# A fifth buffer for the high and the low halves of weights, paid for with two of the 36 large tiles

## The chip, the cores and the metric

One NeuronCore of one Trainium2 chip runs the whole layer in one launch. The metric is device time in microseconds (us) of that core. The kernel before takes 1455.81 us, the median of 3 runs (1452.03 to 1458.66). Engines are named as the profile names them: PE (TensorE), DVE (VectorE), ACT (ScalarE), POOL (GpSimd), SP (SyncE, which issues most loads).

## What is computed

A hybrid decoder layer on x of 1024 tokens by 1024 channels, float32:

```python
h = rmsnorm(x, pre_norm_g) * (1 + scale) + shift          # shift, scale, gate = split(c @ w_ada + b_ada)
q, k, v, z_ret, u_val, u_gate, z_conv, g_a, g_b = split(h @ w_in)     # 1024 x 11264
ret  = head_groupnorm(retention(rotary(q), rotary(k) / 16, v))        # 4 heads, 256 | 512 wide
y_a  = (ret * silu(z_ret)) @ w_ret_out
a    = causal_depthwise_conv(u_val * sigmoid(u_gate), conv_w) + conv_b   # 31 taps
y_b  = (silu(layernorm(a)) * silu(z_conv)) @ w_conv_out
y    = (sigmoid(g_a) * y_a + sigmoid(g_b) * y_b) @ w_out
out  = x + gate * rmsnorm(y, post_norm_g)
```

## The kernel before

**Three products for one.** Each float32 operand is split into a high half, rounded to the PE's fast float32 format, and a low half, the rest. A product is hi x hi + lo x hi + hi x lo. Weights are split on the chip: `load_w` and `load_s` fetch a 128x1024 float32 tile into `ws` (2 buffers), write its high half to `wh` and its low half to `wl`. ACT makes the high half (L124, L128). The low half comes from DVE (`split`, L125) or, in `split_dma`, from ACT, which writes the negated high half (L129), and a DMA issued by POOL that adds the weights onto it (L130).

**The pools.** `whl` gives the buffers of `wh` and of `wl`: 4 each, 4 KB a partition. `unit` gives 36 tiles of the same size to nearly everything large (`U(...)`). `wst` holds `ws` (2), `wa` (1) and three tiles shared under the tag `ld`; `tmp` holds 9 half-size tiles, among them the `p`, `u` and `rt` of a Strassen group. The kernel writes no semaphore: a planner simulates the program, orders each engine's instructions by readiness and by their place in the source, and gives out buffers as they come free. The conv's taps are put 300 places later in that order (`LATER`), so that they fill gaps of DVE. On the chip each engine runs its list in order.

**The projections of `w_in`** are done in 44 groups of 256 output columns, 42 of them by Strassen's scheme (`strassen`, L236): 7 products instead of 8, each product 12 matmuls of 512 columns. A group needs four sets of weights (`load_s`): `wa` for the first product, and three pairs of `wh` and `wl`, each pair read by two products: S1 and S2, then S4 and S3, then 12 and 22. The third pair is split straight from the second `ws` tile, so that the high-half copy (L128) is what frees that `ws` buffer for the next group's load, and the next group's sums x1 and x2 (DVE, L211 to L215) start from that load. Results leave through `evac` functions: a copy from PSUM into a `tmp` tile, sums with other products on DVE, and what the group needs (sigmoid, SiLU, rotary).

**Order of the groups.** Gate and value of the conv branch (`u_groups`, names pg and pu): sigmoid of the gate goes into two unit tiles `sg`, which the value group reads. Then for each of 4 heads: Q, gate a, K, gate b, two groups of V, and for heads 0 and 1 two groups of z (pq, pga, pv, pz). Q and K write their rotary result into two unit tiles `qk` each, which stay until POOL has stored them. Then z of head 2, the layer norm of the conv, z of head 3, and z of the conv (pzc).

**Beside the groups** (`pump`): the rotary tables (`turns`; tiles ang, a1, tacc, tr1, tr2, then sinT and cosT), and the conv: for each of 8 blocks of channels a load `ca`, 31 taps into `co` (L379 and 30 times L385 on DVE, the k-th tap on 1024-k columns), and two stores by POOL (L390, L394).

**Unit tiles through the groups.** The operands of the projections stay from their making to the end of the last group: 16 tiles of h (`hh`, `hl`) and 12 sums of h (`T`), 28 in all. With sinT and cosT it is 30. What is left serves `sg`, the rotary tables' tiles, `ca`, `co` and `qk`.

**After the groups** come the retention by chunks (16 steps, with `w_conv_out` beside it), `w_ret_out`, and `w_out`. These use `whl` by `load_w`, two pairs for each chunk.

Of the kernel before, what the change touches and what calls it, by code (L numbers as in the profile page):

```python
# [68 lines left out]
def block_kernel(ctx: ExitStack, tc: tile.TileContext, x, c, positions, w_ada, w_in, w_ret_out, w_conv_out,  # L69
# [5 lines left out]
    w_ret, w_conv, w_o = w_ret_out, w_conv_out, w_out  # L75

    const = ctx.enter_context(tc.tile_pool(name="const", bufs=1))
    unit = ctx.enter_context(tc.tile_pool(name="unit", bufs=36))
    wst = ctx.enter_context(tc.tile_pool(name="wst", bufs=2))
    whl = ctx.enter_context(tc.tile_pool(name="whl", bufs=4))  # L80
    tmp = ctx.enter_context(tc.tile_pool(name="tmp", bufs=9))
    small = ctx.enter_context(tc.tile_pool(name="small", bufs=2))
    psum = ctx.enter_context(tc.tile_pool(name="psum", bufs=8, space=PSUM))
# [934 lines left out]
```

## Time and profile before

| | |
|---|---|
| three runs | 1455.81, 1452.03, 1458.66 us |
| profiled execution | 1450.67 us, its span 1448.8 us |
| mean granted PE clock | 0.992 |
| busy in the span | PE 96%, DVE 73%, ACT 44%, POOL 13% |
| startup, 0 to 95 us | PE busy 75.52 us |
| `u_groups`, 95 to 228 us | PE busy 130.75 of 133 us |
| heads and first z, 228 to 830 us | PE busy 583.92 of 602 us |
| conv z, 830 to 940 us | PE busy 110.00 of 110 us |

The profile is of one execution. The PE's busy share counts a matmul's time through the array, and neighbours overlap (0.39 us long, 0.227 us apart), so a full row says that PE was never without work, and the number of matmuls in a stretch says how fast it went. In the lists a bracket such as [1.19 <-DMA wl<-in_w_in] is the idle time of that engine just before the instruction and what ended it. In the chain of waits, "issue" is time that no released instruction explains.

### The profile page before, as it was taken

The numbers are of one execution on the slowest core, as the hardware profiler recorded it, in microseconds if no ns is written. First come the engines' busy times: TensorE is split into PE (matmuls) and PEld (weight loads), VectorE is DVE, ScalarE is ACT, GpSimd is POOL, SyncE is SP. The second block draws the span as 40 slices with busy tenths as digits, with TensorE's granted clock in tenths as the row PEclk, the third lists the DMA queues.
The fourth block names the chain that finished last, engine by engine and source line by source line (L and its number), as shares of the span: only waits on it lengthen the run. The fifth ranks groups of instructions, "written<-read, shape, count | busy, mean of one in ns | idle before, by whom it ended". The sixth has DMA issues, their size and how long they took to land.

```text
span 1448.8 us, 17151 instructions
## 1 busy us (share of the span) xinstructions
PE 1397.5 (96%) x6308; PEld 1142.5 (79%) x6308; DVE 1060.8 (73%) x1436; ACT 642.7 (44%) x927; POOL 181.8 (13%) x262
## 2 busy tenths in 40 slices
PE   5899999999999998999999999999999999999998
PEld 2677888788778886788777788878888888888886
DVE  5899999899849994799946876677687756555224
ACT  2655564455455453444455564645354430222121
POOL 2002122121212211121221001010000000000001
PEclk9999999999999999999999999999999999999999
DMA  9227677777787787776896755647766579563403
GB/s 376 72 89 164 144 201 180 196 203 189 191 215 174 183 185 187 198 179 146 198 254 259 256 172 189 223 134 238 253 222 198 166 239 329 181 203 114 146 15 116
DMA packets 113061, 274.46 MB, mean 189 GB/s; under 512 B 10705, under 2 KB 43601, under 8 KB 112978
## 3 DMA queue, kind: packets, MB, share of 16 engines
q1 hardware_dynamic: 77538, 174.62, 36.2%
q0 software_dynamic: 24784, 79.70, 24.8%
q10 hardware_dynamic: 10656, 19.05, 3.5%
q8 instruction: 49, 0.80, 0.2%
q14 instruction: 34, 0.28, 0.1%
HBM read 184.21 MB, written 71.83 MB: 177 GB/s over the span
## 4 chain that ended last, share of the span: by engine, by line
PE 82%; DMA 8%; issue 3%; DVE 3%; ACT 2%; POOL 0%; POOLq 0%; DVEq 0%; SPq 0%; ACTq 0%
PE pgaa L236 5%; PE pva L236 5%; PE pza L236 5%; PE pya L152 4%; PE pya L153 4%; PE pya L154 4%; PE pqa L236 4%; PE pzca L236 3%; PE pzc L236 3%; PE pvc L236 3%; DMA wl<-x 2%; PE pqc L236 2%; DMA wl<-in_w_in 2%; PE py L152 2%; PE py L154 2%
## 5 line engine op out<-in xcount | busy, mean ns | idle before, releaser
L385 DVE SCALAR_TENSOR_TENSOR co<-ca,vec,co 128x1023 f32<-128x1023 f32 (+28 forms) x240 | 298.2, 1264 | 0.3
L124 ACT CAST wh<-ws 128x1024 fp32r<-128x1024 f32 x52 | 54.5, 1049 | 125.4 <-PE pya L153 54.7
L125 DVE TENSOR_TENSOR wl<-ws,wh 128x1024 fp32r<-128x1024 f32 x52 | 63.6, 1222 | 59.2 <-ACT wh L124 59.2
L154 PE MATMUL pya<-rh,wl 128*128 128x512 f32 x256 | 99.7, 389 | 0.0
L153 PE MATMUL pya<-rl,wh 128*128 128x512 f32 x256 | 99.6, 389 | 0.0
L152 PE MATMUL pya<-rh,wh 128*128 128x512 f32 x256 | 98.9, 391 | 0.0
L125 DVE TENSOR_TENSOR wl<-x,wh 128x1024 fp32r<-128x1024 f32 x51 | 62.2, 1221 | 33.4 <-ACT wh L124 25.5
L128 ACT CAST wh<-ws 128x1024 fp32r<-128x1024 f32 x34 | 35.8, 1052 | 84.9 <-PE pqa L236 29.3
L129 ACT ACTIVATE wl<-wh 128x1024 fp32r<-128x1024 f32 x67 | 71.2, 1062 | 0.4
L128 ACT CAST wh<-x 128x1024 fp32r<-128x1024 f32 x33 | 34.8, 1054 | 71.4 <-DVE x L212 52.5
L211 DVE TENSOR_TENSOR x<-ws 128x512 f32<-128x512 f32 x42 | 29.0, 690 | 49.4 <-DMA ws<-in_w_in 49.4
L124 ACT CAST wh<-x 128x1024 fp32r<-128x1024 f32 x51 | 53.4, 1048 | 25.5 <-DVE x L212 11.8
L816 ACT ACTIVATE o<-o,rr 128x512 f32<-128x512 f32 x32 | 24.5, 778 | 84.2 <-DVE rr L814 84.2
L236 PE MATMUL pgaa<-T,wh 128*128 128x512 f32 x192 | 59.6, 392 | 0.4 <-ACT u L242 0.4
L236 PE MATMUL pqa<-T,wh 128*128 128x512 f32 x192 | 59.2, 390 | 0.1
L236 PE MATMUL pza<-T,wh 128*128 128x512 f32 x192 | 59.3, 390 | 0.0
L236 PE MATMUL pva<-T,wh 128*128 128x512 f32 x192 | 59.1, 389 | 0.0
L152 PEld LDWEIGHTS pya<-rh,wh 128*128 128x128 f32 x256 | 48.1, 188 | 10.2 <-ACT wh L124 0.2
L153 PEld LDWEIGHTS pya<-rl,wh 128*128 128x128 f32 x256 | 48.1, 188 | 10.1 <-issue 0.2
L154 PEld LDWEIGHTS pya<-rh,wl 128*128 128x128 f32 x256 | 48.0, 188 | 10.0
L130 POOL DMA_DIRECT2D wl<-x x33 | 28.7, 870 | 216.8 <-ACT wl L129 91.5
L130 POOL DMA_DIRECT2D wl<-in_w_in x34 | 30.0, 882 | 165.5 <-ACT wl L129 136.2
(413 smaller groups left out, 3971.3 us busy)
## 6 DMA issues: line engine op xcount, KB each, us to landing
ws<-in_w_in SPq DMA_DIRECT2D x88, 512.0 KB, 4.3
wl<-in_w_in POOLq DMA_DIRECT2D x34, 512.0 KB, 6.4
wl<-x POOLq DMA_DIRECT2D x33, 512.0 KB, 4.6
wa<-in_w_in POOLq DMA_DIRECT2D x34, 256.0 KB, 5.0
ada<-in_w_ada SPq DMA_DIRECT2D x16, 512.0 KB, 10.2
vr<-v_d SPq DMA_DIRECT2D x16, 512.0 KB, 5.9
ws<-in_w_conv_out SPq DMA_DIRECT2D x16, 512.0 KB, 4.4
szl<-sz_d SPq DMA_DIRECT2D x16, 512.0 KB, 3.8
```

Source lines behind the costliest of these rows:

```text
L124: A.copy(out=hi, in_=src)
L125: lo_eng.tensor_tensor(out=lo, in0=src, in1=f(hi), op=ALU.subtract)
L128: A.copy(out=hi, in_=src)
L129: A.activation(out=lo, in_=f(hi), func=AF.Copy, scale=-1.0)
L130: G.dma_start(out=lo, in_=again, accum_op=ALU.add)
L152: T.matmul(ps, a[0], b[0], start=start and i == 0, stop=False)
L153: T.matmul(ps, a[0], b[1], start=False, stop=False)
L154: T.matmul(ps, a[1], b[0], start=False, stop=stop and i == n - 1)
L211: V.tensor_tensor(out=x1[:, b0], in0=a21, in1=a22, op=ALU.add)
L236: T.matmul(ps, l_[:, k, :], r_, start=start and k == 0 and i == 0, stop=k == 3 and i == 2, skip_group_check=True)
L385: V.scalar_tensor_tensor(out=st["o"][:, s_:], in0=st["a"][:, 0:1024 - s_], scalar=vec[:, i, ROW_CW + k:ROW_CW + k + 1], in1=st["o"][:, s_: ...
L816: A.activation(out=o[:, ib, :], in_=ps, func=AF.Identity, scale=rr[:, 0:1], bias=rr[:, 1:2])
```

## The change

The pool of large tiles gets 34 buffers instead of 36, and `wh` and `wl` get five instead of four. Both take the same memory: two tiles of 4 KB a partition move from the one pool to the other. Nothing else in the source changes; the planner orders the program anew.

```diff
-    unit = ctx.enter_context(tc.tile_pool(name="unit", bufs=36))
+    unit = ctx.enter_context(tc.tile_pool(name="unit", bufs=34))
     wst = ctx.enter_context(tc.tile_pool(name="wst", bufs=2))
-    whl = ctx.enter_context(tc.tile_pool(name="whl", bufs=4))
+    whl = ctx.enter_context(tc.tile_pool(name="whl", bufs=5))
```

## Rows read from the trace of the kernel before

**Rows 1.** Strassen stretches: length, PE busy (matmuls), PEld, DVE, ACT, POOL, clock, DMA, GB/s.
```profile
228.00:386.00 158.00, 155.28 (x683) 127.59 (x682) 147.62 (x165) 80.07 (x109) 29.47 (x38) 1.00 0.73 187
386.00:545.00 159.00, 156.10 (x685) 127.77 (x684) 130.68 (x150) 81.63 (x112) 31.23 (x40) 1.00 0.81 194
545.00:672.00 127.00, 119.77 (x513) 97.42 (x512) 93.78 (x112) 58.65 (x80) 23.39 (x30) 0.97 0.74 185
672.00:830.00 158.00, 152.77 (x658) 122.77 (x657) 117.08 (x146) 76.44 (x107) 25.90 (x35) 1.00 0.76 227
```
**Rows 2.** PE's waits, 95 to 940 us: waited for, total us, times, longest.
```profile
PE pgab L236 <- DMA wl<-in_w_in: 6.0, 3, 4.1
PE pqb L236 <- ACT wh L128: 2.7, 3, 0.9
PE pqc L236 <- DMA wl<-x: 1.8, 1, 1.8
PE pva L236 <- DMA wa<-in_w_in: 1.6, 1, 1.6
PE pgac L236 <- DMA wl<-x: 1.5, 2, 0.8
PE pqa L236 <- DMA wa<-in_w_in: 1.4, 1, 1.4
```
**Rows 3.** ACT in order of time at 386 us: start, us, instruction, [idle before <-releaser].
```profile
386.60 1.05 ACT L128 CAST wh<-ws 128x1024 fp32r<-128x1024 f32 x1 [5.23 <-PE pqa L236]
```
**Rows 4.** Chain of waits there, one product and the transfer: start, us, what.
```profile
401.64 2.72 PE pgaa L236 x12
...
389.49 7.27 DMA wl<-in_w_in
```
**Rows 5.** Chain of waits, 524 to 600 us.
```profile
527.04 1.06 ACT wh L128
...
528.12 3.49 DMA ws<-in_w_in
...
546.32 3.62 issue
...
550.57 9.67 DMA wl<-in_w_in
```
**Rows 6.** The stretch behind that wait, columns as in rows 1.
```profile
560.00:568.00 8.00, 7.71 (x22) 6.14 (x23) 1.63 (x3) 3.16 (x4) 2.21 (x3) 0.63 0.95 240
```
**Rows 7.** DVE in order of time: conv taps and rotary tables in `u_groups`.
```profile
131.62 1.27 DVE L385 SCALAR_TENSOR_TENSOR co<-ca,vec,co 128x1014 f32<-128x1014 f32 x1
...
133.41 1.27 DVE L385 SCALAR_TENSOR_TENSOR co<-ca,vec,co 128x1013 f32<-128x1013 f32 x1
...
144.09 1.22 DVE L464 SCALAR_TENSOR_TENSOR tr<-a,tr 128x1024 f32<-128x1024 f32 x1
...
145.23 0.68 DVE L493 TENSOR_TENSOR p<-pua,sg 128x512 f32<-128x512 f32 x1
...
195.79 1.25 DVE L385 SCALAR_TENSOR_TENSOR co<-ca,vec,co 128x994 f32<-128x994 f32 x1
```
**Rows 8.** ACT in order of time: last product but two of the second value group.
```profile
174.44 0.58 ACT L242 COPY u<-pua 128x512 f32<-128x512 f32 x1
```
**Rows 9.** POOL and SP in order of time: rotary store, conv loads, conv store.
```profile
293.35 0.97 POOL L564 DMA_DIRECT2D k_d<-qk  x1
...
419.42 0.91 SPq L377 DMA_DIRECT2D ca<-a_d  x2
...
719.68 0.56 POOL L390 DMA_DIRECT2D cout_d<-co  x1 [4.31 <-DVE co L385]
```
**Rows 10.** DVE and ACT in order of time: Q, conv and gate a of head 3.
```profile
672.57 0.68 DVE L555 TENSOR_TENSOR qk<-u,cosT 128x512 f32<-128x512 f32 x1
...
673.77 1.26 DVE L385 SCALAR_TENSOR_TENSOR co<-ca,vec,co 128x1003 f32<-128x1003 f32 x1
...
691.89 0.58 ACT L242 COPY u<-pgaa 128x512 f32<-128x512 f32 x1
```
**Rows 11.** The conv's sum: its load, and the matmuls that read it.
```profile
732.88 0.33 SPq L605 DMA_DIRECT2D csum<-csum_d  x1
...
L608 PE MATMUL mean<-csum,onesr x4: 591/592/592, 771.9 to 773.2; 128*128 128x512 f32 x4
```
**Rows 12.** ACT's groups by line, 940 us to the end: busy, mean ns, idle before.
```profile
L124 ACT CAST wh<-ws 128x1024 fp32r<-128x1024 f32 x36 | 37.8, 1049 | 94.4 <-PE pya L153 54.7 <-PE py L154 18.7 <-PE pyb L153 14.8
```

## The prediction

> **What bounds the kernel now.** By the page PE is busy for 1397.5 of 1448.8 us, so only its gaps can be won. I read the busy time by stretches first: from 228 to 830 us, where `whl` serves the Strassen groups, PE lacks work in all four rows, most from 545 to 672 us [rows 1]. How much is lost is read from matmuls, not from the busy share: an undisturbed product of 12 takes 2.72 us [rows 4], 0.2267 us a matmul. 683, 685, 513 and 658 of them would take 154.8, 155.3, 116.3 and 149.2 us; the stretches took 158, 159, 127 and 158, so 3.2 + 3.7 + 10.7 + 8.8 = 26.4 us are lost.
>
> Next, PE's waits: nearly all are for a half of weights [rows 2], 15.0 us in these six rows. Then what made the half late. At 386.60 us ACT copies the third pair's high half, after 5.23 us idle, released by a PE product [rows 3]: it had its `ws` tile and lacked a buffer of `wh`. The low half's transfer starts at 389.49, takes 7.27 us [rows 4], and PE stands before it. The same copy also frees `ws`: at 527.04 it runs, and at 528.12, behind it, the next group's load is issued [rows 5]. So one late buffer makes its own pair late and then the sums, `wa` and the first pair of the next group. Of the twelve waits in rows 2 I put all down to it.
>
> After 940 us the copies wait for buffers even longer, 94.4 us in 36 copies [rows 12], but PE is not what waits: no wait for `wh` or `wl` stands among its waits there. A fifth buffer changes nothing in that part.
>
> **The fifth buffer.** It adds no instruction and no byte. Each pair is read by two products, so the buffer that a copy gets with five was released one pair earlier: two products, 2 x 2.72 = 5.4 us, three where another group's product lies between, 8.2 us. The waits it has to cover are at most 4.1 us, mostly 1 to 2 [rows 2]. Hence, with the shift passed on through `ws`, they go. From the 26.4 us lost I take off what isn't for this buffer: the conv's mean and variance, 8 matmuls that start (773.2 - 771.9) / 3 = 0.43 us apart [rows 11], 8 x (0.43 - 0.227) = 1.6 us; and about 5 us for waits outside rows 2 (a `wl` whose `ws` load itself landed late, PSUM copies, the first zc pair). 20 us remain. 2.7 of them are no wait: behind the wait of 4.1 us PE runs at a granted clock of 0.63 over 8 us [rows 6], that is at 1.2 instead of 2.4 GHz for most of them, and does 22 matmuls where 35 fit; (35 - 22) x 0.2267 = 2.9. They go if the wait goes.
>
> That longest wait has a second cause: POOL stood 3.62 us ("issue") before a conv store, and the low half's transfer at 550.57 was queued behind it [rows 5]. Nothing in the change moves it, so I take only part of that wait, and leave 2 us. Gain: 20 - 2 = 18 us; bounds 0 (something else is as late) and 22.
>
> What is late next? The two `ws` buffers and the one of `wa` stay. `wa` is read by a group's first product alone and so is free for most of a group (7 products, 19 us); I take nothing for it.
>
> The Trainium skill, "DMA: Bandwidth & Descriptors", section "Issuing engines are not separate DMA queues", says that transfers issued by SP, ACT and POOL run on the same 16 engines and interleave. This case shows the like: the late low half took 9.67 us against 7.27 [rows 4, 5]. By that rule alone an earlier start would buy little where the engines are full; that is the first rival below.
>
> **The 34 large tiles.** 28 hold the operands until the last group, 30 with sinT and cosT, so 6 were left and 4 are. Who is short depends on how the planner gives them out. After the store at 293.35 two of 36 are free, yet the next conv loads, which need only old data, are issued at 419.42, two at once, beside K of head 1 [rows 9]. I read from this that tiles are given out in source order: nobody overtakes an earlier tile that hasn't been written. With that the ledger can be kept by hand.
>
> *`u_groups`, 8 left before, 6 after.* ca, co, ang, a1, the first sg tile and tr1 take them. tacc is next and must wait for the first sg tile's last read, about 142 us; the second sg tile must wait behind it for a buffer of the conv, that is for the last tap. Already before, this pool was short: the rotary tables' write at 144.09 comes right after a value group's read had freed a tile [rows 7]. Now the taps: the 10th is at 131.62, the 11th 1.79 later, about the least spacing of one chain, since other DVE work hides in it [rows 7]. The rotary work is out of the way, so 20 taps at 1.8 to 2.0 us end at 168 to 172 us, against 195.79 + 1.25 before. PE can run on meanwhile: the sigmoid holds back 6 of the 9 `tmp` tiles (one and two of the first gate and value group, three of the second gate group), three are left for the second value group, and the copy at 174.44 is the first without one [rows 8]. 172 plus two DVE reads is about 174. I take 3 us of PE's time for this; bounds 0, and, if the taps ended as late as before, 197 + 2 - 174.4 = 25 us.
>
> *Heads.* Two conv channels need 4 tiles and Q or K 2: 6, all that was left. With 4, the second channel starts only after K's stores, some 20 us late, and Q of the next head waits for the first channel's end. For head 3: at 673.77 both channels are at their 21st tap of 30 (1003 columns) [rows 10]. The total of 41 is what DVE manages, so it stays, but shifted: the first channel has had some ten alone, so it is at 25 and the second at 15. 5 more taps each, 10 at about 2 us, put the first one's end at 693, and Q's first rotary write goes from 672.57 to about 694. Q then holds 6 `tmp` tiles (two sums, two copies, two rt), gate a the other 3; its next copy, at 691.89 [rows 10], waits to about 695. I take 3 us; bounds 0, and, if the channel ended only at 719 as before [rows 9], 720 + 2 - 691.9 = 30. At head 1 the same count gives Q a wait of some 10 us, less than the 19 that gate a gives; at head 2 none.
>
> *After.* The conv ends perhaps 10 us later; its sum was loaded at 732.88 and first read at 771.9 [rows 11], cover of over 30 us. Without that cover the delay would come on PE one for one. In the conv z groups six b tiles wait for earlier ones, in the retention and behind it tiles are free many us before they are written: nothing.
>
> **Sum.** Profiled execution 1450.67 - 18 + 3 + 3 = 1438.7 us. That execution lies 5.1 us under the median of 1455.81, so I expect 1443.8 us in runs like the three: 1444, -0.8%. Its own range is 1437 to 1449.
>
> **Rivals.**
> *The DMA engines are the bound.* For: 9.67 us to land before the longest wait [rows 5], DMA engines busy for 0.73 to 0.81 of all four stretches [rows 1]. Against: the transfers are the same, and 5 to 8 us of lead exceed their stretch of some 2.4 us. Then the longest wait and its clock remain (4.1 + 2.9), and some 4 us of the others; gain 18 - 9 = 9 less 6 for the tiles: 1453, no change that a measurement tells.
> *Large tiles stop PE.* One mechanism: a tile held by the conv keeps back sg or Q's rotary tiles until `tmp` runs out. It decides where the first channel's last tap comes after 174 us in `u_groups`, or after about 692 in head 3. Priced at the upper bounds, 25 to 30 us at one place, with the gain of 18 kept: 1455.8 - 18 + 28 = 1466. For: both places come out within 3 us of the edge. Against: the taps have the lowest rank and get whatever DVE has free, which is more when others wait.
> *All waits go and tiles cost nothing*: 1455.8 - 22 = 1434.
> That the fifth buffer isn't used can't be: copies find none free in nearly every group.
>
> **Chances.** Forecast 0.5, DMA engines 0.2, large tiles stop PE 0.18, everything goes 0.12. A run tells 0.5%, 7.3 us, from no change: under 1448.5 is faster, over 1463.1 slower. Faster: 0.5 x 0.84 + 0.2 x 0.1 + 0.12 = 0.56. Slower: 0.18 x 0.75 = 0.14, and 0.01 for the rest. Same: 0.29. The range that leaves out 0.2 is 1431 to 1461: it holds the first two cases and the last, and the smaller prices of the third.
>
> **What would show it.** Right: rows 2's waits gone or under 1 us, the L128 copy with hardly any idle released by PE, the clock at 1.00 in every stretch behind 228 us; tacc written after 142 us; conv loads one by one instead of two at once; Q's rotary writes of head 3 after the first channel's store. Wrong: low halves that start earlier and still land as PE needs them (DMA engines); PE idle between 174 and 200 us or around 690 behind an ACT copy or a sigmoid (large tiles). If two conv channels still start together, tiles aren't given out in source order, and the costs for tiles are none.

## The result, and the profile after

The changed kernel takes 1470.39 us (median of 7 runs, 1461.96 to 1474.69) against 1455.81 (7 runs on the same chip): ratio 1.0102, 95% interval 1.0084 to 1.0121. That is 14.6 us slower, where 1444 was forecast with a range of 1431 to 1461. The profiled execution took 1474.69 us, its span is 1473.0 (before 1450.67 and 1448.8). It is the slowest of its seven runs, and the one profiled before lies 5 us under its median, so what the two traces differ by, 24.2 us, is more than the 14.6 of the medians.

The four Strassen stretches of the changed kernel, by windows (columns as in [rows 1]):

```profile
228.00:386.00 158.00, 147.77 (x633) 120.42 (x632) 134.51 (x150) 75.14 (x101) 28.46 (x37) 0.98 0.70 175
386.00:545.00 159.00, 153.55 (x668) 125.71 (x667) 136.24 (x154) 81.11 (x110) 29.11 (x37) 0.99 0.75 189
545.00:672.00 127.00, 119.00 (x503) 96.68 (x502) 93.93 (x110) 59.03 (x81) 23.62 (x30) 0.96 0.74 186
672.00:830.00 158.00, 152.39 (x664) 124.16 (x663) 123.67 (x145) 77.35 (x105) 27.52 (x39) 1.00 0.76 220
```

By the same sum as for [rows 1], 633, 668, 503 and 664 matmuls of 0.2267 us fill 143.5, 151.4, 114.0 and 150.5 us. 14.5 + 7.6 + 13.0 + 7.5 = 42.6 us are lost, against 26.4 before. Taken from the starts of single matmuls between 95 and 940 us, 36.9 us more than the usual 0.2267 us each lie in gaps of over 0.9 us (before 20.4), and 18.1 in spacings of 0.3 to 0.9 us (before 11.3); 50 of these 86 spacings are of about 0.43 us, matmuls at half the clock. What both grew by is together 23 us, all but 1 of the 24.2 by which the span grew. Behind 940 us nothing changed, as forecast: the long gaps there sum to 4.1 us (before 4.7).

PE's waits in the changed kernel, 95 to 940 us (columns as in [rows 2]):

```profile
PE pvb L236 <- DMA wl<-in_w_in: 14.3, 4, 4.4
PE pqb L236 <- DMA wl<-in_w_in: 6.5, 4, 2.8
PE pqc L236 <- DMA wl<-x: 4.7, 3, 3.5
PE pvc L236 <- DMA wl<-x: 4.1, 2, 2.3
```

The same kind of wait as in [rows 2], but 29.6 us in four rows instead of 15.0 in six. 20.8 of it lie at `pvb` and `pqb` (before 6.0 + 2.7 at `pgab` and `pqb`): in bank b a group sums its product 12 x 21, and it waits for the low half of the third pair.

One such wait, on PE in order of time (start, us, instruction, idle before and its releaser):

```profile
303.83 0.39 PE L236 MATMUL pvb<-hh,wh 128*128 128x512 f32 x1
304.05 0.39 PE L236 MATMUL pvb<-hl,wh 128*128 128x512 f32 x1
...
314.27 0.50 PE L236 MATMUL pvb<-hh,wl 128*128 128x512 f32 x1 [4.39 <-DMA wl<-in_w_in]
...
339.83 0.39 PE L236 MATMUL pva<-T,wl 128*128 128x512 f32 x1
```

PE begins 12 x 21 with the two matmuls that need the high half, does other products, and comes back for the low half before it has landed. The last matmul that reads this pair ends at 339.83 + 0.39 = 340.22, that is 36 us after the first began at 303.83. Two products alone take 5.4 us. The clock pays too: the granted clock is 0.79 over the 8 us around the wait.

```profile
312.00:320.00 8.00, 5.73 (x18) 4.58 (x19) 6.34 (x7) 4.99 (x8) 2.24 (x3) 0.79 0.64 169
```

ACT at the same place, in order of time:

```profile
301.08 1.05 ACT L128 CAST wh<-ws 128x1024 fp32r<-128x1024 f32 x1 [3.50 <-PE pgaa L236]
302.03 0.58 ACT L242 COPY u<-pgaa 128x512 f32<-128x512 f32 x1
302.93 1.25 ACT L379 ACTIVATE co<-ca,vec 128x1024 f32<-128x1024 f32 x1 [0.32 <-issue]
304.08 1.04 ACT L129 ACTIVATE wl<-wh 128x1024 fp32r<-128x1024 f32 x1
...
310.63 1.24 ACT L379 ACTIVATE co<-ca,vec 128x1024 f32<-128x1024 f32 x1 [3.87 <-DMA ca<-a_d]
```

The copy of the high half still waits for a PE product, that is for a buffer, although there are five, as in [rows 3]. Between it and the copy that starts the low half (L129) stands the first write of a conv sum (L379), which needs a large tile. Here it costs little: without it L129 could have begun behind L242, at 302.61 instead of 304.08. The rest of the way from the copy at 301.08 to the landing at 305.55 + 8.68 = 314.23 is the copies and the transfer. The chain from there to PE:

```profile
294.08 8.53 DMA csum_d<-co
302.61 0.32 issue
302.93 0.04 ACT co L379
...
304.08 1.05 ACT wl L129
...
305.55 8.68 DMA wl<-in_w_in
```

By this chain the tile came free when a conv sum's accumulating store landed, 8.53 us after its issue. What ACT waited for at L379 in all, first in the kernel before, then in the changed one (the line view: waited for, us, times):

```profile
  DMA ca<-a_d: 0.3, 1
  DMA csum_d<-co: 0.2, 1
```

```profile
  DMA ca<-a_d: 13.4, 3
  DMA k_d<-qk: 9.4, 2
  issue: 0.3, 1
```

From 0.5 to 23.1 us. The prediction doesn't name this wait; what it is worth is tried in e5 and e6.

The ledger of tiles, on the other hand, came out in its order as worked out. DVE in order of time, tables, last tap of conv 0, Q of head 3:

```profile
148.78 1.22 DVE L464 SCALAR_TENSOR_TENSOR tacc<-a,tr 128x1024 f32<-128x1024 f32 x1
...
176.46 1.25 DVE L385 SCALAR_TENSOR_TENSOR co<-ca,vec,co 128x994 f32<-128x994 f32 x1
...
719.62 0.69 DVE L555 TENSOR_TENSOR qk<-u,cosT 128x512 f32<-128x512 f32 x1
...
727.00 0.69 DVE L555 TENSOR_TENSOR qk<-p,cosT 128x512 f32<-128x512 f32 x1 [1.92 <-DMA csum_d<-co]
```

and SP's conv loads, one by one where [rows 9] had two at once:

```profile
291.86 0.33 SPq L377 DMA_DIRECT2D ca<-a_d  x1
...
305.18 0.33 SPq L377 DMA_DIRECT2D ca<-a_d  x1
```

### The profile page after: what moved, and what is told of

Same layout as the page of the kernel before. It is cut to its first block, busy times and chain, and to the rows that moved or that the text cites. A ratio compares the mean times of both kernels' runs of the same rounds, so it can differ in the third digit from the quotient of the medians.

```text
span 1473.0 us, 17158 instructions
## 1 busy us (share of the span) xinstructions
PE 1407.5 (96%) x6308; PEld 1149.8 (78%) x6308; DVE 1063.4 (72%) x1436; ACT 644.8 (44%) x927; POOL 182.2 (12%) x262
## 4 chain that ended last, share of the span: by engine, by line
PE 76%; DMA 10%; issue 5%; DVE 4%; ACT 3%; POOL 1%; ACTq 0%; POOLq 0%; DVEq 0%; SPq 0%
DMA wl<-in_w_in 5%; PE pza L236 5%; PE pva L236 5%; PE pya L152 4%; PE pya L153 4%; PE pya L154 4%; PE pqa L236 3%; PE pgaa L236 3%; PE pzca L236 3%; PE pvc L236 3%; PE pzc L236 2%; DMA ws<-in_w_in 2%; PE py L154 2%; PE py L152 2%; PE pqc L236 2%
## 5 line engine op out<-in xcount | busy, mean ns | idle before, releaser
L385 DVE SCALAR_TENSOR_TENSOR co<-ca,vec,co 128x1001 f32<-128x1001 f32 (+28 forms) x240 | 299.1, 1264 | 10.7 <-ACT co L379 10.1
L124 ACT CAST wh<-ws 128x1024 fp32r<-128x1024 f32 x52 | 54.5, 1051 | 118.2 <-PE pya L153 60.3
L124 ACT CAST wh<-x 128x1024 fp32r<-128x1024 f32 x51 | 53.6, 1050 | 58.2 <-PE pgaa L236 17.6
L129 ACT ACTIVATE wl<-wh 128x1024 fp32r<-128x1024 f32 x67 | 71.2, 1062 | 0.8
L128 ACT CAST wh<-ws 128x1024 fp32r<-128x1024 f32 x34 | 35.8, 1054 | 51.7 <-PE pgaa L236 29.8
L128 ACT CAST wh<-x 128x1024 fp32r<-128x1024 f32 x33 | 34.9, 1056 | 49.7 <-DVE x L212 37.9
L152 PEld LDWEIGHTS pya<-rh,wh 128*128 128x128 f32 x256 | 48.1, 188 | 10.2 <-issue 0.2
L152 PE MATMUL pyb<-bh,wh 128*128 128x512 f32 x128 | 50.0, 391 | 0.0
```

The source lines that it names most:

```text
L124: A.copy(out=hi, in_=src)
L128: A.copy(out=hi, in_=src)
L129: A.activation(out=lo, in_=f(hi), func=AF.Copy, scale=-1.0)
L152: T.matmul(ps, a[0], b[0], start=start and i == 0, stop=False)
L385: V.scalar_tensor_tensor(out=st["o"][:, s_:], in0=st["a"][:, 0:1024 - s_], scalar=vec[:, i, ROW_CW + k:ROW_CW + k + 1], in1=st["o"][:, s_: ...
```

## The experiments

Two counts go with every kernel, taken from the order of its instructions, not from times. *In use*: matmuls from the first to the last that reads a low half made by DMA. *Lead*: matmuls from the last that read the former content of the pair's buffers (of the high and the low one, that released later) to the first that reads this low half. Both are medians of some 63 halves, PE's 480th to 3750th matmul. What the lead has to cover can be read from [rows 3, 4]: from the start of the copy at 386.60 to the landing at 389.49 + 7.27 = 396.76 are 10.2 us, 45 matmuls. In the changed kernel's wait above it is 314.23 - 301.08 = 13.2 us, 58 matmuls.

| kernel | tiles | `wh`/`wl` | in use | lead | us | ratio to before (95%) |
|---|---|---|---|---|---|---|
| before | 36 | 4 | 59 | 59 | 1455.8 | 1 |
| changed | 34 | 5 | 95 | 46 | 1470.4 | 1.0102 (1.0084-1.0121) |
| e1 | 34 | 4 | 59 | 51 | 1468.3 | 1.0098 (1.0080-1.0117) |
| e2: 7 tmp, 2 ld | 36 | 4 | 59 | 60 | 1471.6 | 1.0125 (1.0105-1.0145) |
| e3: 7 tmp, 2 ld | 36 | 5 | 96 | 55 | 1455.6 | 1.0007 (0.9991-1.0023) |
| e4 | 35 | 4/5 | 59 | 50 | 1452.2 | 0.9987 (0.9971-1.0004) |
| e5: conv on DVE | 34 | 5 | 95 | 48 | 1459.9 | 1.0028 (1.0013-1.0042) |
| e6: conv on DVE | 36 | 4 | 59 | 51 | 1446.3 | 0.9937 (0.9918-0.9956) |
| e7: 7 tmp | 35 | 5 | 93 | 49 | 1457.3 | 1.0021 (1.0007-1.0034) |
| e8: 7 tmp | 36 | 4 | 59 | 59 | 1452.4 | 0.9986 (0.9970-1.0003) |
| e9: 2 held early | 36 | 4 | 57 | 60 | 1461.8 | 1.0044 (1.0028-1.0061) |
| e10: 2 held late | 36 | 4 | 59 | 49 | 1460.5 | 1.0038 (1.0022-1.0054) |
| e11: 6 tmp, packed | 36 | 5 | 93 | 56 | 1447.4 | 0.9953 (0.9935-0.9970) |
| e12: 6 tmp, packed | 36 | 4 | 59 | 59 | 1451.4 | 0.9974 (0.9960-0.9989) |
| e13: bank c | 34 | 5 | 35 | 101 | 1450.7 | 0.9980 (0.9967-0.9992) |
| e14: bank c | 36 | 4 | 33 | 88 | 1441.4 | 0.9919 (0.9895-0.9942) |
| e15: bank c, 6 tmp, packed | 36 | 5 | 33 | 101 | 1438.8 | 0.9900 (0.9882-0.9918) |
| e16: bank c, conv on DVE | 36 | 4 | 34 | 87 | 1441.9 | 0.9915 (0.9896-0.9935) |
| e17: as e15, conv on DVE | 36 | 5 | 33 | 101 | 1444.2 | 0.9922 (0.9897-0.9947) |
| e18: as e14, 6 tmp, packed | 38 | 4 | 33 | 77 | 1445.7 | 0.9934 (0.9911-0.9958) |

The lead in the table is a median over two kinds of halves, about as many of each, and falls now on the one, now on the other. Counted apart, the third pair (12 and 22, the one waited for in bank b) has a lead of 60 to 62 in every kernel with four buffers of `wh` (e4 too), of 46 to 49 with five, of 97 with four and bank c, of 127 to 130 with five and bank c. The first pair (S1 and S2) has 49 or 50, 59 to 69, 49, and 61 to 63. So the table's 49 to 60 among the kernels with four buffers tell of no difference. And five buffers take some 13 matmuls of lead from the half that PE waits for, and give 10 to 20 to the other.

**One part at a time (e1 to e4).** The tiles alone:

```diff
-    unit = ctx.enter_context(tc.tile_pool(name="unit", bufs=36))
+    unit = ctx.enter_context(tc.tile_pool(name="unit", bufs=34))
```

> 34 large tiles with four weight buffers, so the tiles alone. Counted in the order of the instructions: a DMA-made low half is read first 51 matmuls after its buffer was released (before 59, changed kernel 46), and stays in use for 59 (before 59, changed kernel 95). Theory 'order' (the planner spends the fifth buffer on working further ahead, holds each buffer longer, and with few tiles lets the low halves come late): small loss, 1456 to 1461 us. Rival 'tiles' (the missing two tiles stop ACT at the conv's first write and with it the weight copies): nearly the whole loss, 1467 to 1472. Rival 'buffer' (the fifth buffer alone does it): as before, 1453 to 1458.

1468.3: the rival 'tiles'. The tiles alone cost 14 us, nearly the whole loss; my first theory, that order makes it, had given them 0 to 5. In e1's trace PE does 24 matmuls fewer than before from 95 to 228 us and 39 fewer from 228 to 830, that is 5.4 and 8.8 us.

For the buffer alone its 8 KB must come from elsewhere. First from small tiles, with a control:

```diff
-    tmp = ctx.enter_context(tc.tile_pool(name="tmp", bufs=9))
+    tmp = ctx.enter_context(tc.tile_pool(name="tmp", bufs=7))
-        return wst.tile([P, 1024], F32, name=name, tag="ld", bufs=3)
+        return wst.tile([P, 1024], F32, name=name, tag="ld", bufs=2)
```

> Control for the next run: 36 large tiles, four weight buffers, but 7 instead of 9 tmp tiles and 2 instead of 3 ld tiles, which is the memory that a fifth buffer needs. Distance 60, in use for 59 matmuls, as before. Theory 'order': no change, 1453 to 1460 us. If tmp or ld tiles matter by themselves, it is slower, and the next run is read against this one.

> 36 large tiles and five weight buffers, paid for with 2 tmp tiles and 1 ld tile: the fifth buffer alone, against the control. In use for 96 matmuls as in the changed kernel, but distance 55. Theory 'order': 2 to 5 us over the control. Rival 'buffer': 12 to 18 us over the control. Rival 'tiles', and my prediction's gain for the buffer (18 us): 10 to 18 us under the control.

The control itself lost 18 us, and with the fifth buffer 16 of them came back. That looks like the gain of my forecast, but only over a kernel that having two `ld` tiles instead of three had made slow (e8 shows that it was these). Why a fifth buffer makes up for an `ld` tile isn't shown: the counts move here as they do with three `ld` tiles (e11, e12), where it gains little. e4 gave the low halves alone a fifth buffer, for one tile:

```diff
-        lo = whl.tile([P, 1024], F32R, name="wl", tag="wl")
+        lo = whl.tile([P, 1024], F32R, name="wl", tag="wl", bufs=5)
```

> 35 large tiles, a fifth buffer for the low halves only. In use for 59 matmuls as before; a low half's own buffer is free 86 matmuls ahead, its high half's only 50. Theory 'order': what counts is the high half's buffer, as the low half is made from it, so 1456 to 1462 us. If a low half needs only its own buffer, 1440 to 1450. Rival 'tiles': about half of the loss, 1461 to 1466.

1452.2, no change that can be told, between what the first two theories gave; whether a little gain and a little loss cancel here isn't settled.

**Is it ACT that stands at the conv's first write? (e5, e6)** Against the changed kernel and the one before:

```diff
-            A.activation(out=st["o"], in_=a, func=AF.Identity, scale=vec[:, i, ROW_CW + 30:ROW_CW + 31],
-                         bias=vec[:, i, ROW_CB:ROW_CB + 1])
+            with tc.high_priority(offset=-LATER):
+                V.tensor_scalar(out=st["o"], in0=a, scalar1=vec[:, i, ROW_CW + 30:ROW_CW + 31],
+                                scalar2=vec[:, i, ROW_CB:ROW_CB + 1], op0=ALU.mult, op1=ALU.add)
```

> The changed kernel (34 tiles, five buffers) with the first write of each conv channel's sum on DVE, at the taps' low rank, instead of on ACT. In the trace of the changed kernel ACT stands before this write for 23.1 us in 6 places, for a large tile to come free (before: 0.5 us), and the weights' copies stand behind it. Theory 'ACT stands': a good part of the loss goes, 1456 to 1464 us. Rival: DVE stands there instead and holds the sums of weights just as long, or the wait held back nothing: 1466 to 1475.

> Control: the kernel before (36 tiles, four buffers) with the same move of the conv's first write to DVE. With tiles at hand ACT waits for nothing there, so both theories: no change, 1452 to 1460 us.

The changed kernel gained 10.5 us, but the kernel before, where ACT waits there for 0.5 us and no change was expected, gained 9 as well; why isn't shown. The gap between them stayed, 13.7 us. So the wait at L379 doesn't explain the loss as I held; in e5 DVE took it over for 10.0 us (the view of waits, at the same instruction, now on DVE):

```profile
DVE co L380 <- DMA ca<-a_d: 6.4, 2, 5.3
DVE co L380 <- issue: 3.6, 1, 3.6
```

This pair doesn't rule out that an engine's standing for a tile costs time, whichever engine it is.

**What do tmp tiles and a 35th tile count? (e7, e8)** Against the kernel before, e8 is the first line alone, e7 all three:

```diff
+    tmp = ctx.enter_context(tc.tile_pool(name="tmp", bufs=7))
+    unit = ctx.enter_context(tc.tile_pool(name="unit", bufs=35))
+    whl = ctx.enter_context(tc.tile_pool(name="whl", bufs=5))
```

> 35 large tiles, five buffers for both halves, 7 tmp tiles, 3 ld tiles. Theory 'the fifth buffer is worth 16 us where tiles suffice' (36 tiles: 1455.6 against 1471.6 with four), and 35 tiles lose little: 1438 to 1449 us. Rival 'tiles dose' (half of the loss of 34 tiles, 7 us, and no gain for the buffer once a tile is missing): 1458 to 1465. If it was the 7 tmp tiles that cost the 16 us in the control: 1452 to 1460.

> The kernel before with 7 instead of 9 tmp tiles: which half of the control's 16 us is it? If tmp: 1465 to 1473 us. If the ld tiles (the waits that grew in the control are for copies of sums that lie in ld tiles): 1452 to 1459. I hold the second likelier.

7 `tmp` tiles cost nothing (1452.4), so e2's loss goes back to its 2 `ld` tiles. With them out of the way five buffers and 35 tiles gain nothing (1457.3): the hope from e3 fell. That lies just under the range of 'tiles dose', too.

**Where do missing tiles cost? (e9, e10)** Two of 36 tiles are taken, and let go at a set point: from before the second gate group until the cosine table is written (e9), or from then until the conv's mean is (e10). The edit of e9:

```diff
+    held = [U(name="held") for _ in range(2)]
+    for d in held:
+        G.memset(d[:, 0:1], 0.0)
     u_groups(1, ws_)
...
     while "cos" not in tr:
         pump(0.0, 5.0)
+    for d in held:
+        V.tensor_tensor(out=d[:, 0:1], in0=d[:, 0:1], in1=tr["cos"][:, 0:1], op=ALU.mult)
```

> 36 tiles, four buffers; two large tiles are taken before the second gate group and let go when the cosine table is written (about 200 us): the shortage of 34 tiles in the gate and value groups alone. Adds two tiny instructions on POOL and two on DVE. 34 tiles throughout, with four buffers, cost 14 us. My prediction's price for this place: 3 us, so 1456 to 1461. If the shortage acts mostly here (late rotary tables, ACT's copies bunched behind them): 1463 to 1469. If it acts in the heads: 1453 to 1457.

> 36 tiles, four buffers; two large tiles are taken when the cosine table is written and let go when the conv's mean is (about 770 us): the shortage in the heads alone. Adds four tiny DVE instructions. A low half's distance from its buffer's release is 49 matmuls here (before 59, 34 tiles 51, two held in the gate and value groups 60). My prediction's price for this place: 3 us, 1456 to 1461. Theory 'in the heads': 1463 to 1470 us. If the other place makes the loss: 1453 to 1457.

Ratios 1.0044 and 1.0038: 6.4 and 5.5 us. Both places count, and together (12) they make nearly all of e1's 14. Each by itself is not far from my price of 3 us: e10 lies in the range written for it, e9 just above. ACT in e9, in order of time:

```profile
173.33 0.63 ACT L488 ACTIVATE sg<-u 128x512 f32<-128x512 f32 x1 [6.22 <-DVE co L385]
...
174.34 1.04 ACT L128 CAST wh<-ws 128x1024 fp32r<-128x1024 f32 x1
```

The sigmoid stands 6.22 us for the tile that the last tap frees, as the ledger said. The copy behind it in ACT's queue is a weight's, but it comes only 0.85 us later than in the kernel before (173.49), and PE waits for nothing there. PE pays later, when the rotary tables are done (cosT at 205.78, before 190.64). POOL and PE there:

```profile
215.94 0.58 POOL L494 DMA_DIRECT2D a_d<-u  x1 [8.78 <-DVE u L493]
216.65 0.87 POOL L130 DMA_DIRECT2D wa<-in_w_in  x1
...
222.95 1.22 PE L236 MATMUL pgaa<-hh,wa 128*128 128x512 f32 x2 [4.99 <-DMA wa<-in_w_in]
```

POOL stands 8.78 us at the store of a value group's result, as it stood before a conv store in [rows 5]. Behind it in POOL's queue is the transfer for `wa`, whose negated half ACT had finished at 214.12; so the store put it off by 2.5 us, and PE waits 4.99 us for its landing. e1 has the same wait, 4.35 us at 223.07. ACT in e10, at Q of head 3:

```profile
705.77 0.59 ACT L242 COPY p<-pqc 128x512 f32<-128x512 f32 x1 [5.53 <-DMA sga_d<-u]
...
707.25 1.06 ACT L128 CAST wh<-x 128x1024 fp32r<-128x1024 f32 x1 [0.40 <-ACT p L572]
713.42 0.58 ACT L242 COPY u<-pqa 128x512 f32<-128x512 f32 x1 [5.11 <-DMA sga_d<-p]
713.90 1.06 ACT L129 ACTIVATE wl<-wh 128x1024 fp32r<-128x1024 f32 x1
```

Here `tmp` has run out, the mechanism of my second rival: two PSUM copies wait for a sigmoid's store. Between L128 and L129 of one pair lie 5.6 us, 5.11 of them standing. POOL issues this pair's transfer at 715.37, behind L129, and PE waits 3.13 us for its landing:

```profile
720.22 0.50 PE L236 MATMUL pgac<-hh,wl 128*128 128x512 f32 x1 [3.13 <-DMA wl<-x]
```

**The fifth buffer with all ld tiles (e11, e12).** Three `tmp` tiles and packed constants pay for it (the mask in bf16, unused columns of `cst` dropped, small tiles put into others):

```diff
-    tmp = ctx.enter_context(tc.tile_pool(name="tmp", bufs=9))
+    tmp = ctx.enter_context(tc.tile_pool(name="tmp", bufs=6))
-    cmask = const.tile([P, P], F32, name="cmask")
+    cmask = const.tile([P, P], mybir.dt.bfloat16, name="cmask")
-NCONST = 40
+NCONST = 19
...
```

> 36 large tiles and five buffers with all 3 ld tiles: paid for with 3 tmp tiles and by packing small constants (the causal mask in bf16). Theory 'the planner spends the buffer on working ahead': a DMA-made half is in use for 93 matmuls (with four 59) and is read 56 after its buffer's release (with four 59), so no gain: within 4 us of the control. My prediction's gain of 18 us, which 36 tiles and 2 ld tiles seemed to bear out: 14 to 20 us under the control, 1436 to 1442.

> Control for the last: four buffers, 36 large tiles, 6 tmp tiles, the same packed constants. 7 tmp tiles cost nothing (1452.4), so 1451 to 1459 us; if the sixth is where tmp tiles begin to count, 1460 to 1470.

1447.4 against 1451.4: 4 us, with intervals that just overlap, not 18. So the fifth buffer gains 4 us or less. ACT's group of third-pair copies, 95 to 940 us, with five buffers, then with four (idle before them and what ended it):

```profile
L128 ACT CAST wh<-ws 128x1024 fp32r<-128x1024 f32 x34 | 35.8, 1052 | 33.3 <-PE pgaa L236 16.0 <-PE pqa L236 8.7 <-PE pza L236 4.3
```

```profile
L128 ACT CAST wh<-ws 128x1024 fp32r<-128x1024 f32 x34 | 35.8, 1053 | 91.4 <-PE pqa L236 30.7 <-PE pgaa L236 18.5 <-PE pva L236 14.4
```

The copies do wait less, by 58 us. PE hardly gains, as in the planner's new order the products start earlier too: in use rises from 59 to 93, and the lead of the third pair falls from 60 to 48.

**Holding product 12 x 21 to its turn (e13, e14, e15).** `pb` had a bank of its own, so this product could start as soon as its high half was there. Summed in bank c it has to follow S4 x 22:

```diff
-        pa, pc, pb = PS(name + "a"), PS(name + "c"), PS(name + "b")
+        pa, pc = PS(name + "a"), PS(name + "c")
+        pb = pc
```

> The changed kernel (34 tiles, five buffers), but each group's product 12 x 21 is summed in bank c, free again behind S4 x 22, instead of a bank of its own, so it can't be placed ahead of its turn. Counted in the order of the instructions a DMA-made low half is now in use for 35 matmuls (changed kernel 95) and first read 101 after its buffer's release (46). Theory 'early 12 x 21' (the planner starts this product as soon as its high half is there, holds the buffer until the last product, and PE stands before the low half): most of the 33 us of waits for halves go; the loss for tiles stays: 1438 to 1452 us. Rival 'bank': PE waits for DVE's read of bank c before 12 x 21, 1 us or more in each of 36 groups, 1470 to 1500. Rival 'transfers are the bound': waits for low halves stay, 1464 to 1474.

> The kernel before (36 tiles, four buffers) with the same edit: in use for 33 matmuls (before 59), first read 88 after the release (before 59). The path from release to landing takes some 12 us, about 54 matmuls, so four buffers then suffice. Theory 'early 12 x 21': the 15 us of waits for halves go, 1436 to 1446 us. Rivals as in the last: 1455 to 1490, or as before.

> 36 tiles, five buffers, 6 tmp tiles and packed constants, with the same edit: first read 101 matmuls after the release. If what the fifth buffer lacked was its lead (88 is already enough with four): no gain over the last run, within 4 us of it, 1434 to 1446. If the fifth buffer's value was held back by the planner's order: 10 us or more under the last.

e13 and e14 fell within what 'early 12 x 21' gave, and e15 within the range for a fifth buffer that adds nothing: 1450.7, 1441.4, 1438.8. The one line takes 1.2% from the changed kernel and 0.8% from the one before. The stretches of e14 by windows, and PE's waits, the first three and the longest for a low half, 95 to 940 us:

```profile
228.00:386.00 158.00, 155.62 (x680) 128.16 (x679) 146.02 (x163) 80.01 (x110) 28.79 (x37) 0.99 0.76 189
386.00:545.00 159.00, 156.64 (x682) 128.54 (x681) 133.67 (x153) 81.86 (x111) 30.13 (x39) 0.99 0.78 193
545.00:672.00 127.00, 124.27 (x541) 102.13 (x540) 100.04 (x118) 63.01 (x85) 26.54 (x34) 0.99 0.80 197
672.00:830.00 158.00, 156.76 (x682) 127.60 (x681) 119.05 (x146) 80.41 (x111) 24.62 (x34) 1.00 0.78 236
```

```profile
PE pgaa L236 <- ACT u L242: 3.8, 3, 1.3
PE pua L236 <- DMA wa<-in_w_in: 2.5, 1, 2.5
PE pgaa L236 <- ACT wa L128: 2.3, 2, 1.5
...
PE puc L236 <- DMA wl<-x: 1.1, 1, 1.1
```

By the sum of [rows 1] the four stretches lose 3.8 + 4.4 + 4.4 + 3.4 = 16.0 us, before 26.4. The long waits for low halves are gone (1.6 us in the whole list of e14), with the DMA engines busy for 0.76 to 0.80, before 0.73 to 0.81. In e14 the third pair's lead is 97 with four buffers, against the 45 to 58 that a half needed above; the fifth (e15) then adds 2.6 us, the two intervals overlap, and e15's smaller pools and constants alone were worth some 4 (e12). The edit also leaves a group two of PSUM's banks instead of three. That is hardly where the gain comes from: PE's waits for copies out of PSUM sum to 0.7 us before and to 5.3 in e14.

**Put together (e16 to e18).** e16 adds e5's edit to e14, e17 to e15. e18 is e15 with the fifth buffer's 8 KB given to two more tiles.

> The kernel before with both edits that speak for themselves: 12 x 21 in bank c, and the conv's first write on DVE (by itself -9 us, 1446.3). If the two gains add up: 1426 to 1438 us. If both take away the same waits: 1438 to 1446.

> 36 tiles, five buffers, 6 tmp tiles, packed constants, 12 x 21 in bank c, and the conv's first write on DVE. With four buffers that last edit added nothing (1441.9 against 1441.4). If so here too: 1435 to 1443 us. If a shorter ACT queue helps where halves come early: 1428 to 1435.

> The memory of the fifth buffer given to large tiles instead: 38 of them, four buffers, 6 tmp tiles, packed constants, 12 x 21 in bank c. 34 against 36 tiles cost 14 us. If tiles are still short at 36: 1430 to 1437. If 36 are enough (ACT stands before the conv's first write for 9 us in two places with 36): as with 36, 1437 to 1445.

1441.9, 1444.2 and 1445.7: the gains of e6 and e14 don't add up, and with 12 x 21 in its turn 38 tiles gain nothing over 36. e17 and e18 lie about 1 us above the higher of their ranges. e15 is the fastest measured, 1.0% under the kernel before.

## Why the prediction was wrong

*Lost time and its kind* held: PE loses 26 us in the four stretches, its listed waits are nearly all for weights, and e14, where those for halves are gone, is 12 us faster (10.4 by the sum of the stretches). Small slips change nothing: the waits in [rows 2] are eleven, not twelve, and 1.79 us is not the least spacing of taps, as four of them take 5.15 us at 161.16 in the changed kernel.

*The fifth buffer* is the step that failed. "the buffer that a copy gets with five was released one pair earlier: two products, 2 x 2.72 = 5.4 us" took PE's order as given. The order is the planner's, and with five buffers it is another one: halves stay in use for 93 to 96 matmuls instead of 59 (changed kernel, e3, e11), and the third pair's lead, which should have grown by 24, falls from 61 to 46 in the changed kernel (48 in e11). 61 covers the 45 to 58 matmuls that the way to a landing took in the two places above; 46 and 48 lie within them. 18 us were forecast; e11 against e12 shows 4, and the changed kernel against e1 none (2 us slower, 0.6 by their ratios). e13 and e14 bear out that it is the order: they forbid one product to start early, the third pair's lead rises to 97 and more, and both are faster, with five buffers and with four. Five buffers in the order of four were not run. Why the planner takes this product so early isn't shown.

*The tiles* are the second step that failed: they were followed correctly in order and priced too low, 6 us for 14. Source order, the tables' start after 142 us (148.78), single conv loads and Q behind the first channel's end are as forecast. Conv 0 ended at 177.7 where 168 to 172 stood, and the first channel of head 3 at about 718, the upper bound, where 693 stood. The price was sought at PE's next PSUM copy, 3 + 3 us; measured are 6.4 + 5.5 (e9, e10) and 14 together (e1). The prediction asked who waits for the late tile, and not who is queued behind the one who waits. In e10 a PSUM copy stands on ACT, with a weight copy behind it, and in e9 a store stands on POOL, with a weight transfer behind it. ACT in the changed kernel at head 3:

```profile
719.63 0.58 ACT L242 COPY u<-pgaa 128x512 f32<-128x512 f32 x1 [4.58 <-DMA sga_d<-p]
720.74 0.59 ACT L242 COPY p<-pqa 128x512 f32<-128x512 f32 x1 [0.53 <-DMA sga_d<-u]
721.22 1.05 ACT L128 CAST wh<-x 128x1024 fp32r<-128x1024 f32 x1
```

The Trainium skill, "PSUM — Partial Sum Buffer", section "Engine vs sequencer instructions", says that the queues of ScalarE, VectorE and GpSimdE are strictly first in, first out; the rows of e10 and e9 agree (L129 behind 5.11 us of standing, the transfer for `wa` behind 8.78). In the rows just shown the copy at 721.22 lost at most 1.5 us, since the sum it reads was written until 719.01 + 0.68 = 719.69. How the 14 us divide among the places where ACT, DVE and POOL stand is not settled: e5 and e6 took away one of them and moved the gap by 1 us only.

*The sum.* The forecast of 1443.8 us missed by 26.6: 14 for the buffer (4 instead of 18), 8 for the tiles (14 instead of 6), and 4.6 more. -4 for the buffer and +14 for the tiles give +10; measured is +14.6. The rest may be the two together, or the error of the terms, whose intervals are some 2.5 us to either side; no run tells. With 12 x 21 in its turn, 34 against 36 tiles still cost 8 to 12 us (e13 against e15: 11.9, of which some 4 may be e15's smaller pools and constants, as e12 is a little faster than the kernel before).

*The rivals.* 'Large tiles stop PE' (1466, chance 0.18) came nearest in time, and e10 shows its beginning, `tmp` running out; but PE lost the time through late weights and in many places, not 28 us in one. With the buffer's gain of 18 in its sum, its time is in part luck. 'The DMA engines are the bound' fell: e14 moves the same bytes with a DMA share of 0.76 to 0.80 and without the waits. The rule of the Trainium skill on shared DMA engines ("DMA: Bandwidth & Descriptors", section "Issuing engines are not separate DMA queues"), named in the prediction, gives no bound here.

## What to carry to other kernels

Where a planner sets the order, one more buffer is not one more step of lead: count in the new order how long each buffer is in use and how far its release lies ahead of the next read, before a gain is put down. Where a pool gets smaller, list the instructions that will wait for it and look at what stands behind each on its engine, here weight copies on ACT and a weight transfer on POOL. A product that may start early on half of its operands holds a buffer and can make PE stand for the other half; here, tying it to the bank of a product before it was worth more (12 us) than the buffer (4).

## What else the runs showed

Two instead of three `ld` tiles cost some 19 us (e2 against e8: 1471.6 and 1452.4). In e2 PE waits 6.6 and 3.6 us for high halves made at L124 (before 1.1 us in all). And by the chain in the section on the result, a large tile came free only when the accumulating store of a conv sum had landed, 8.53 us after its issue.
